# Strassen-Winograd FFN layer: token halves exchanged in the down projection, product order, hat tiles and row scaling moved

## The chip, the cores and the metric

One Trainium2 chip, one of its cores. The metric is the device time of one launch in microseconds, as the median of repeated runs. TensorE, VectorE, ScalarE, GpSimd and SyncE appear in the profile as PE (with its weight loads as PEld), DVE, ACT, POOL and SP; SP issues nearly all of the DMAs.

## The reference, cut to what matters

One decoder layer on 1024 tokens of width 1024, in float32:

```
h = h + 0.5 * post1(SwiGLU_1(pre1(h)))     FFN 1, hidden width 2816
h = h + postM(Mixer(preM(h)))              attention + linear recurrence
h = h + 0.5 * post2(SwiGLU_2(pre2(h)))     FFN 2, hidden width 2816
swiglu(x) = (silu(x @ w_gate) * (x @ w_up)) @ w_down
```

pre and post are RMS norms with a gain per column. The change touches the two FFNs, and, through one shared routine, the row scaling of the normed residual in FFN 1 and in the mixer.

## The kernel before, in words

**Products.** Every float32 product is three matmuls: each operand is split into a high half (ACT, a rounding copy, line 132) and a low half (DVE, a subtraction, line 133), and hi*hi, hi*lo, lo*hi are accumulated (lines 153 to 155). The split tiles are called hats; `wh` is a ring of 6 such tiles, `wr` a ring of 4 raw weight tiles, `hx` a ring of 6 raw hidden tiles.

**Strassen-Winograd.** Each FFN matrix product is cut in two along tokens, inner width and output width, and done in 7 products instead of 8. With A11, A12 the first and A21, A22 the second token half, and B the weight:

- s1 = A21 + A22, s2 = s1 - A11, s3 = A11 - A21, s4 = A12 - s2; t1 = B12 - B11, t2 = B22 - t1, t3 = B22 - B12, t4 = B21 - t2.
- P1 = A11 B11, P2 = A12 B21, P3 = s4 B22, P4 = A22 t4, P5 = s1 t1, P6 = s2 t2, P7 = s3 t3.
- C11 = P1 + P2, C12 = P1 + P5 + P6 + P3, C21 = P1 + P6 + P7 + P4, C22 = P1 + P5 + P6 + P7.

P1, P2 and P3 use a weight block as it is ("raw"); the others need a weight sum first (`wsum`, line 324: DVE, or DVE and POOL in turn).

**Stages.** FFN 1 runs from 0 to about 690 us, the mixer to about 1430, FFN 2 to the end. In an FFN, `hidden` (line 442) loops over 11 column tiles f and, for gate and up (m = 0, 1), over `unit` (line 380), which makes the four quarters of the hidden, S[h, j] for token half h and width half j. `early` does P1 and P2 of some units beforehand. A unit's seven products are in the order P1, P5, P2, P6, P3, P7, P4, the first two perhaps done early. P6, P7 and P4 go on in the PSUM tile `c` that P5 began. At the end the unit writes the A-operands of the down projection to DRAM: hid[0] to hid[6] hold A11, A12, s4, A22, s1, s2, s3. Before the change A11, A12 are S[0, 0], S[0, 1], and A22 is S[1, 1].

`down` (line 456) frees the pools of the hidden stage and opens its own over them; pool `hp` (`hx` and weight sums) lies where pool `xc` lay. `products` (line 480) runs P1, P2, then P5 and P6 together, P3, P7, P4, each as a loop over 11 f with 12 matmuls of 512 columns an f (24 in the P5/P6 loop). The token halves' rows are f1[0], f1[1]; L and R are their left and right 512 columns. f1[0] is complete after P3; then a generator `side` is stepped once per f beside P7 and P4: the six steps of `residual` (line 167: square on ACT, `rsqrt` on DVE and POOL, gain and addition on DVE, store, second norm with the row scaling of line 188 on DVE), and in FFN 1 eight steps of `to_T` (transposes on PE into a PSUM tile `pa`, a split each). FFN 2 ends with class `Last`: P4's weights and hats are split in the P3 and P7 loops into tiles of their own (`wl`, `xl`), and `rows` (line 592) then does P4 one 128-token tile after another, 33 matmuls each, with the post norm and the store of each beside the next.

**What sets the order.** The program is a list; the framework's list scheduler orders each engine's queue when the kernel is built, by program order and by a simulated time at which an instruction becomes ready, and adds the semaphores. A pool that lies over an older one counts as ready, for that ordering, when the older pool's last reader is through. At run time each engine, and SP with its DMAs, takes its queue strictly in order.

Of the kernel before, what the change touches and what calls it, by code (L numbers as in the profile page):

```python
# [16 lines left out]
D = 1024  # L17
# [28 lines left out]
def layer(ctx: ExitStack, tc: tile.TileContext, I: dict, out: bass.AP):  # L46
# [172 lines left out]


    hid = dram.tile([7, NP, 128, HT], F32, name="hid")
    spill = dram.tile([max(EARLY.values()), 2, 128, HT], F32, name="spill")
    spill_a = dram.tile([4, 128, 2, HT], F32, name="spill_a")
    turn = [0]

    class Ffn:
# [124 lines left out]

        def out(self, S, m, f, i, h, j, c):

# [4 lines left out]
            else:  # L358
                tt(S[h, j], S[h, j], c, op=OP.mult)
                nc.sync.dma_start(hid[i - 1, f], S[h, j])  # L360

        def early(self):

            for f in range(self.early_tiles):
# [10 lines left out]
                for m in range(2):  # L375
                    yield from self.prod_steps(2, r[m][0][:, 1], q[m], False)
                    self.out(S, m, f, 1, 0, 0, q[m])
                    yield

        def unit(self, f, m, S):  # L380

# [18 lines left out]
            if first:  # L400
                self.prod(2, b21, q, False)
                self.out(S, m, f, 1, 0, 0, q)
            else:
                if m == 0:
                    S[0, 0] = self.place(0, 0)
                    nc.sync.dma_start(S[0, 0], hid[0, f])
                yield
# [12 lines left out]
            tt(y, c, p1, op=OP.add)  # L420
            self.out(S, m, f, 4, 1, 1, y)
            t4 = self.wsum(b21, t2, OP.subtract, ESUM)
            yield
            self.prod(4, t4, c, False)
            tt(e, c, e, op=OP.add)
            if m == 0:
                nc.scalar.activation(e, e, AF.Silu)
                return
            tt(S[1, 0], S[1, 0], e, op=OP.mult)

            s1, s2, s4 = (self.at.tile([128, HT], F32, name=n) for n in ("s1", "s2", "s4"))
            s3 = S[1, 0]
# [3 lines left out]
            nc.sync.dma_start(hid[6, f], s3)  # L436
            tt(s2, s1, S[0, 0], op=OP.subtract)
            nc.sync.dma_start(hid[5, f], s2)
            tt(s4, S[0, 1], s2, op=OP.subtract)
            nc.sync.dma_start(hid[2, f], s4)  # L440

        def hidden(self):
# [3 lines left out]
            for f in range(NP):  # L446
                S = {}
                for m in range(2):
                    u = self.unit(f, m, S)
                    next(u)  # L450
# [29 lines left out]
        def products(self, f1, done, beside, last):  # L480


            Wd = self.Wd
            T2 = [self.wl.tile([128, 512], F32, name=f"t2_{f}", tag=f"xl{f}") for f in range(NP)]

# [33 lines left out]

            side = iter(())  # L520

            def raws(acc, i, b, start):
                for f in range(NP):
                    x = halves(xhat(i, f))
                    mul(acc, x, halves(blocks(f, b)[b]), f, start)

            pa = [ptile("pa") for _ in range(4)]
            raws(pa, 1, (0, 0), True)
            for t in range(4):
                nc.scalar.activation(L(1, t), pa[t], AF.Copy)  # L530
            raws(pa, 2, (1, 0), False)
            for t in range(4):
                nc.scalar.activation(L(0, t), pa[t], AF.Copy)
            pa, pb = ([ptile(tag) for _ in range(4)] for tag in ("pa", "pb"))
# [12 lines left out]
            pa = [ptile("pa") for _ in range(4)]  # L547
            for f in range(NP):
                x = halves(xhat(3, f))
                W = blocks(f, (1, 1), (1, 0)) if last else blocks(f, (1, 1))  # L550
                mul(pa, x, halves(W[1, 1]), f)
                if last:
                    last.weights(f, self.wsum(W[1, 0], T2[f], OP.subtract, 2))
            for t in range(4):
                tt(R(0, t), pa[t], R(0, t), op=OP.add)
            side = then(done(), beside)
            for f in range(NP):
                x = halves(xhat(7, f))
                W = blocks(f, (0, 1), (1, 1))
                mul(pb, x, halves(self.wsum(W[1, 1], W[0, 1], OP.subtract, 2)), f, False)  # L560
                if last:
                    last.inner(f, xhat(4, f))
                next(side, None)
            for t in range(4):
                tt(R(1, t), pb[t], R(1, t), op=OP.add)
            if last:
                last.rows(f1[0], f1[1], pb, side)
                return
            for f in range(NP):
                x = halves(xhat(4, f))  # L570
                W = blocks(f, (1, 0))
                mul(pb, x, halves(self.wsum(W[1, 0], T2[f], OP.subtract, 2)), f, False)
                next(side, None)
            run(side)
            for t in range(4):
                tt(L(1, t), pb[t], L(1, t), op=OP.add)

    class Last:
# [4 lines left out]

        def weights(self, f, s):
            w = self.w[f] = self.ffn.wl.tile([128, 2, 512], F32R, name=f"wl{f}")
            split(w[:, 0], w[:, 1], s)

        def inner(self, f, s):
            x = self.x[f] = self.ffn.wl.tile([128, 2, 512], F32R, name=f"xl{f}")
            split(x[:, 0], x[:, 1], s)  # L590

        def rows(self, x, m, acc, side):
            src, dst, g = self.ffn.src, self.ffn.dst, self.g
            run(side)
            head = []
# [10 lines left out]
            for t in range(4):  # L606
                p = acc[t]
                for f in range(NP):
                    mm3(p, cols(self.x[f], t), (self.w[f][:, 0], self.w[f][:, 1]), f == 0, f == NP - 1, False)
                L = m[t][:, :512]  # L610
# [38 lines left out]
    rp = pool(sr1, "r1")  # L649
    rows0 = [F1.xb.tile([128, D], F32, name="xrow0", tag=f"xh6_{t}") for t in range(4)]  # L650
    load_rows(rows0, 0)
# [14 lines left out]
    def to_T(pl, rows, res, tag):  # L666
        for dt in range(8):
# [8 lines left out]
    f1, res1, srp, sf1, sf0 = F1.down(lambda: xT.append(pool(sxta, "xta", side="right")),  # L676
                                      lambda rows: to_T(xT[2], rows, xT[0], "pa"))
    sf0.close()
# [641 lines left out]
```

## Time and profile before

| | |
|---|---|
| median of 3 runs | 2028.68 us (2025.11 to 2029.44) |
| the profiled execution's own time | 2022.87 us |
| its span | 2021.1 us |
| PE busy | 1914.3 us, 95% |
| DVE, ACT, POOL busy | 70%, 48%, 29% |
| mean granted TensorE clock | 0.977 |

The profile's page gives busy shares for the whole span; the questions here are about stretches of 5 to 60 us, so the trace is read by windows, by the timeline of one engine, and by tile. A granted clock of 1.00 is 2.4 GHz, 0.50 is 1.2 GHz; the mean of a window lies between when the clock was low for part of it.

### The profile page before, as it was taken

The page shows a single profiled execution, that of the slowest core. Times are in us where ns is not written, and L with a number is a line of the kernel's source. Part 1 is how long each engine was busy: PE and PEld are TensorE (multiplying, and loading weights), DVE is VectorE, ACT ScalarE, POOL GpSimd, SP SyncE. Part 2 cuts the span into 40 slices and gives each one's busy share as a digit, 9 for nine tenths or more (in the row PEclk, how much of TensorE's full clock was granted, in tenths as well). Part 3 has the DMA queues.
Part 4 walks back from the last instruction along what each step waited for, and adds up shares of the span by engine and source line. Part 5 has one row for each costly group of instructions (what it writes and reads, how often), then busy time and mean ns, then how long its engine had stood idle before and what let it go on. Part 6 is the DMA issues. An engine that isn't in the chain of part 4 may idle for free.

```text
span 2021.1 us, 26939 instructions
## 1 busy us (share of the span) xinstructions
PE 1914.3 (95%) x9034; PEld 1566.8 (78%) x9034; DVE 1413.3 (70%) x2515; ACT 966.7 (48%) x1887; POOL 579.9 (29%) x549
## 2 busy tenths in 40 slices
PE   7999999999998989899999999988989999989988
PEld 5788888877886766688787878877868888868876
DVE  5777766655759865856885785754787788756794
ACT  7423333324444536458886676754633222224451
POOL 1433212200004444155534431223233332310131
PEclk9999999999999999999999999999989999999999
DMA  6554333236859453563323253134745455457694
GB/s 218 168 157 154 102 110 110 94 108 221 287 166 309 113 164 95 153 170 87 122 93 113 87 162 123 64 113 126 241 152 162 146 163 174 135 198 255 207 308 136
DMA packets 290107, 316.54 MB, mean 157 GB/s; under 512 B 19920, under 2 KB 200240, under 8 KB 289968
## 3 DMA queue, kind: packets, MB, share of 16 engines
q1 hardware_dynamic: 289392, 312.72, 49.1%
q0 software_dynamic: 576, 2.10, 0.3%
q8 instruction: 71, 1.16, 0.2%
q14 instruction: 68, 0.56, 0.1%
HBM read 237.62 MB, written 74.97 MB: 155 GB/s over the span
## 4 chain that ended last, share of the span: by engine, by line
PE 67%; DVE 12%; DMA 8%; issue 7%; ACT 5%; POOL 1%; SPq 0%; DVEq 0%; POOLq 0%; ACTq 0%
PE pa L154 10%; PE pa L155 10%; PE pa L153 10%; PE pb L155 4%; PE pb L154 4%; PE pb L153 4%; PE pj L153 4%; PE pj L154 4%; PE pj L155 4%; PE av L1105 3%; PE pt L1118 3%; DVE wh L133 3%; DMA wr<-in_ffn_w_down 3%; PE sc L1056 1%; PE sc L1055 1%
## 5 line engine op out<-in xcount | busy, mean ns | idle before, releaser
L153 PE MATMUL pa<-xh,wh 128*128 128x512 f32 x728 | 284.7, 394 | 11.6 <-ACT xh L132 4.6
L154 PE MATMUL pa<-xh,wh 128*128 128x512 f32 x728 | 286.0, 393 | 0.7 <-DVE xh L133 0.7
L155 PE MATMUL pa<-xh,wh 128*128 128x512 f32 x728 | 281.3, 392 | 0.0
L132 ACT ACTIVATE wh<-ws 128x512 fp32r<-128x512 f32 x231 | 143.3, 626 | 267.2 <-PE pa L155 193.2
L133 DVE TENSOR_TENSOR wh<-wr,wh 128x512 fp32r<-128x512 f32 (+1 forms) x248 | 195.3, 792 | 60.2 <-ACT wh L132 59.2
L132 ACT ACTIVATE wh<-wr 128x512 fp32r<-128x512 f32 (+1 forms) x248 | 152.7, 621 | 133.8 <-PE pa L155 80.1
L324 POOL TENSOR_TENSOR ws<-wr 128x512 f32<-128x512 f32 x54 | 79.7, 1476 | 389.6 <-DVE wh L133 249.1
L133 DVE TENSOR_TENSOR wh<-ws,wh 128x512 fp32r<-128x512 f32 x231 | 188.2, 816 | 4.0 <-ACT wh L132 2.9
L132 ACT ACTIVATE wh<-hx 128x512 fp32r<-128x512 f32 x143 | 90.1, 630 | 209.6 <-PE pa L155 117.1
L153 PEld LDWEIGHTS pa<-xh,wh 128*128 128x128 f32 x728 | 137.7, 189 | 42.9 <-ACT xh L132 4.8
L1072 POOL TENSOR_SCALAR s<-s,cf 128x64 f32<-128x64 f32 (+4 forms) x192 | 117.3, 634 | 185.6 <-DVE cf L1068 127.1
L133 DVE TENSOR_TENSOR wh<-hx,wh 128x512 fp32r<-128x512 f32 x143 | 105.3, 736 | 84.6 <-ACT wh L132 84.3
L154 PEld LDWEIGHTS pa<-xh,wh 128*128 128x128 f32 x728 | 137.7, 189 | 30.3 <-DVE xh L133 1.7
L155 PEld LDWEIGHTS pa<-xh,wh 128*128 128x128 f32 x728 | 137.8, 189 | 29.2
L154 PE MATMUL pa<-wh 128*128 128x512 f32 x352 | 139.2, 395 | 4.2 <-DVE wh L133 4.2
L143 POOL TENSOR_TENSOR wh<-wr,wh 128x512 fp32r<-128x512 f32 (+1 forms) x74 | 101.9, 1388 | 137.4 <-ACT wh L142 134.5
L155 PE MATMUL pa<-wh 128*128 128x512 f32 x352 | 138.7, 394 | 0.0
L153 PE MATMUL pj<-xT,wh 128*128 128x512 f32 (+1 forms) x304 | 124.1, 412 | 13.2 <-DVE gq L913 5.1
L153 PE MATMUL pb<-xh,wh 128*128 128x512 f32 x328 | 128.9, 393 | 0.0
L155 PE MATMUL pb<-xh,wh 128*128 128x512 f32 x328 | 128.6, 393 | 0.0
L154 PE MATMUL pb<-xh,wh 128*128 128x512 f32 x328 | 128.3, 391 | 0.0
L133 DVE TENSOR_TENSOR PT<-pt,PT 128x512 fp32r<-128x512 f32 (+3 forms) x184 | 104.4, 578 | 29.4 <-ACT PT L132 28.6
(360 smaller groups left out, 4629.5 us busy)
## 6 DMA issues: line engine op xcount, KB each, us to landing
hx<-hid SPq DMA_DIRECT2D x154, 256.0 KB
wr<-in_ffn_w_down SPq DMA_DIRECT2D x132, 256.0 KB
wr<-in_ffn_w_gate SPq DMA_DIRECT2D x60, 512.0 KB
wr<-in_ffn_w_up SPq DMA_DIRECT2D x60, 512.0 KB
hid<-S SPq DMA_DIRECT2D x88, 256.0 KB
wr<-in_w_in SPq DMA_DIRECT2D x36, 512.0 KB
hid<-s SPq DMA_DIRECT2D x66, 256.0 KB
wr<-in_ffn_w_down SPq DMA_DIRECT2D x33, 512.0 KB
```

Of the source, the lines that this page charges most:

```text
L132: nc.scalar.activation(hi, src, AF.Copy)
L133: tt(lo, src, hi.bitcast(F32), op=OP.subtract)
L143: nc.gpsimd.tensor_tensor(lo, src, hi.bitcast(F32), op=OP.subtract)
L153: nc.tensor.matmul(p, a[0], b[0], start=start and fresh, stop=False, skip_group_check=not fresh)
L154: nc.tensor.matmul(p, a[0], b[1], start=False, stop=False, skip_group_check=not fresh)
L155: nc.tensor.matmul(p, a[1], b[0], start=False, stop=stop, skip_group_check=not fresh)
L324: (nc.vector if turn[0] % every == 0 else nc.gpsimd).tensor_tensor(s, a, b, op=op)
L1055: nc.tensor.matmul(p[:, :b - a], Q[:, 0, ts], rhs[:, a:b], start=True, stop=False)
L1056: nc.tensor.matmul(p[:, :b - a], Q[:, 1, ts], rhs[:, a:b], start=False, stop=True)
L1072: nc.gpsimd.tensor_scalar(S[k, br][:, :n], S[k, br][:, :n], cf[:, k, br:br + 1], 1.0, op0=OP.mult, op1=OP.mult)
L1105: nc.tensor.matmul(av[:, k0 * 128:(k0 + nk) * 128], lhs, PT[:npart, y, at:at + nk * 128], start=(wi == 0 and y == 0), stop=(wi == len(work ...
L1118: nc.tensor.transpose(pt[:npart, at:at + 128], S[k, br][:, (j - lo_) * npart:(j - lo_ + 1) * npart], idt)
```

## The change

- The token halves exchange roles in the down projection: A11, A12 are S[1, 0], S[1, 1], and A21, A22 are S[0, 0], S[0, 1]. hid[0] is written at the end of each unit; what `early` makes goes to a DRAM tensor of its own, hid0, and S[0, 0] of a unit that was not begun early is not stored.
- `products` now runs P1, (P5, P6), P7, P4, P3, P2. f1[0] is complete after P4. `side` is stepped beside P3 and P2, and `to_T` uses PSUM tiles `pb`; P3 and P2 accumulate in `pa`.
- In FFN 2, `Last.rows` finishes P2: its first 6 f run as a plain loop, the last 5 (`LATE`) are split in the P3 loop into own tiles and are done by token tile, 15 matmuls each.
- In the very last unit of the hidden stage P4 goes to a PSUM tile of its own, with one more DVE addition.
- Hats of P4's operand move from pool `xc` to `xb`, those of P6's from `xb` to `xc`.
- The row scaling of `residual` is an ACT copy with a scale instead of a DVE multiplication.

```diff
@@ residual
-                nc.vector.tensor_scalar(f[t], f[t], r[t], None, op0=OP.mult)
+                nc.scalar.activation(f[t], f[t], AF.Copy, scale=r[t])
@@ build1
-                self.hat(self.xc, 4, k, B[k + 4])
+                self.hat(self.xb, 4, k, B[k + 4])
...
-                self.hat(self.xb, 6, k, s2)
+                self.hat(self.xc, 6, k, s2)
@@ out
-                nc.sync.dma_start(hid[i - 1, f], S[h, j])
+                if to is not None:
+                    nc.sync.dma_start(to, S[h, j])
@@ unit
-            self.out(S, m, f, 2, 0, 1, x)
+            self.out(S, m, hid[3, f], 0, 1, x)
...
-            self.out(S, m, f, 4, 1, 1, y)
+            self.out(S, m, hid[1, f], 1, 1, y)
+            if last:
+                tt(e, c, e, op=OP.add)
+                c = either(self.tags)
             t4 = self.wsum(b21, t2, OP.subtract, ESUM)
             yield
-            self.prod(4, t4, c, False)
+            self.prod(4, t4, c, last)
             tt(e, c, e, op=OP.add)
+            self.out(S, m, hid[0, f], 1, 0, e)
...
-            nc.gpsimd.tensor_tensor(s1, S[1, 0], S[1, 1], op=OP.add)
+            nc.gpsimd.tensor_tensor(s1, S[0, 0], S[0, 1], op=OP.add)
...
-            nc.gpsimd.tensor_tensor(s3, S[0, 0], S[1, 0], op=OP.subtract)
+            nc.gpsimd.tensor_tensor(S[0, 0], S[1, 0], S[0, 0], op=OP.subtract)
...
-            tt(s2, s1, S[0, 0], op=OP.subtract)
+            tt(s2, s1, S[1, 0], op=OP.subtract)
...
-            tt(s4, S[0, 1], s2, op=OP.subtract)
+            tt(s4, S[1, 1], s2, op=OP.subtract)
@@ products (after the P5/P6 loop; the new order)
             for t in range(4):
-                tt(R(1, t), pa[t], L(1, t), op=OP.add)
+                tt(R(0, t), pa[t], L(1, t), op=OP.add)
             for t in range(4):
-                tt(R(0, t), pb[t], R(1, t), op=OP.add)
...
+                tt(R(1, t), pb[t], R(0, t), op=OP.add)
             for f in range(NP):
                 x = halves(xhat(7, f))
                 W = blocks(f, (0, 1), (1, 1))
                 mul(pb, x, halves(self.wsum(W[1, 1], W[0, 1], OP.subtract, 2)), f, False)
...
             for t in range(4):
-                tt(R(1, t), pb[t], R(1, t), op=OP.add)
...
+                tt(R(0, t), pb[t], R(0, t), op=OP.add)
             for f in range(NP):
                 x = halves(xhat(4, f))
                 W = blocks(f, (1, 0))
                 mul(pb, x, halves(self.wsum(W[1, 0], T2[f], OP.subtract, 2)), f, False)
+            for t in range(4):
+                tt(L(0, t), pb[t], L(1, t), op=OP.add)
+            side = then(done(), beside)
+            pa = [ptile("pa") for _ in range(4)]
+            late = range(NP - LATE if last else NP, NP)
+            for f in range(NP):
+                mul(pa, halves(xhat(3, f)), next_w((1, 1), f), f)
+                if f in late:
+                    last.ready(f, xhat(2, f), blocks(f, (1, 0))[1, 0])
+                next(side, None)
+            for t in range(4):
+                tt(R(1, t), pa[t], R(1, t), op=OP.add)
+            pa = [ptile("pa") for _ in range(4)]
+            for f in range(late[0] if last else NP):
+                mul(pa, halves(xhat(2, f)), next_w((1, 0), f), f)
                 next(side, None)
             run(side)
+            if last:
+                last.rows(f1[0], f1[1], pa, late)
+                return
             for t in range(4):
-                tt(L(1, t), pb[t], L(1, t), op=OP.add)
+                tt(L(1, t), pa[t], L(1, t), op=OP.add)
```

## Rows read from the trace of the kernel before

**Rows 1.** The profile's page, part 1: busy us (share of the span) xinstructions.

```profile
span 2021.1 us, 26939 instructions
...
PE 1914.3 (95%) x9034; PEld 1566.8 (78%) x9034; DVE 1413.3 (70%) x2515; ACT 966.7 (48%) x1887; POOL 579.9 (29%) x549
```

**Rows 2.** Windows of 25 us; the columns are named in the first line.

```profile
core 0: us, PE busy (x) PEld busy (x) DVE busy (x) ACT busy (x) POOL busy (x), PEclk, DMA share, GB/s
425.00:450.00 25.00, 24.12 (x106) 19.51 (x105) 11.48 (x18) 4.91 (x8) 0.51 (x1) 1.00 0.30 102
450.00:475.00 25.00, 21.11 (x83) 16.39 (x82) 13.89 (x20) 9.11 (x16) 3.50 (x2) 0.86 0.79 263
...
600.00:625.00 25.00, 23.42 (x103) 18.73 (x102) 20.14 (x29) 11.74 (x22) 8.84 (x7) 1.00 0.92 313
625.00:650.00 25.00, 19.39 (x85) 14.84 (x84) 24.85 (x35) 14.04 (x26) 12.01 (x9) 0.98 0.88 298
...
675.00:700.00 25.00, 21.32 (x82) 16.95 (x81) 19.37 (x39) 9.59 (x18) 14.71 (x14) 0.86 0.26 64
...
1775.00:1800.00 25.00, 18.70 (x70) 14.01 (x69) 14.52 (x20) 5.54 (x10) 2.87 (x2) 0.86 0.69 243
...
1925.00:1950.00 25.00, 25.00 (x112) 20.71 (x111) 22.19 (x33) 16.30 (x29) 7.89 (x5) 1.00 0.90 307
1950.00:1975.00 25.00, 19.39 (x76) 14.85 (x75) 25.00 (x36) 12.36 (x24) 8.33 (x7) 0.93 0.89 301
1975.00:2000.00 25.00, 23.71 (x105) 19.32 (x104) 10.20 (x19) 5.49 (x14) 5.59 (x5) 1.00 0.48 158
```

**Rows 3.** Timeline of PE where the hidden stage ends: start, us, operation, [idle before <-releaser].

```profile
449.33 0.47 PE L153 MATMUL pa<-xh,wh 128*128 128x512 f32 x1 [0.88 <-DVE cy L420]
...
454.35 1.91 PE L153 MATMUL pa<-wh 128*128 128x512 f32 x4 [2.05 <-ACT wh L132]
458.10 0.80 PE L154 MATMUL pa<-wh 128*128 128x512 f32 x1 [1.84 <-DVE wh L133]
...
1778.85 0.47 PE L153 MATMUL pa<-xh,wh 128*128 128x512 f32 x1 [0.87 <-DVE cx L410]
```

**Rows 4.** Timeline of SP's DMA queue at the same two places.

```profile
438.30 11.97 SPq L360 DMA_DIRECT2D hid<-S  x3
450.35 2.77 SPq L507 DMA_DIRECT2D hx<-hid  x6
...
1783.74 2.78 SPq L507 DMA_DIRECT2D hx<-hid  x6
```

**Rows 5.** Timeline of PE in P4, at the mixer's first matmul, and in P7.

```profile
649.57 0.77 PE L153 MATMUL pb<-wh 128*128 128x512 f32 x1 [4.05 <-DVE f L565]
...
687.54 0.77 PE L153 MATMUL pj<-xT,wh 128*128 128x512 f32 x1 [3.67 <-DVE f L576]
...
1962.05 0.50 PE L154 MATMUL pb<-wh 128*128 128x512 f32 x1 [3.29 <-DVE wh L133]
```

**Rows 6.** Line 188, row scaling: ns min/median/max; then what its engine waited for.

```profile
L188 DVE TENSOR_SCALAR f<-f,r x8: 737/752/1789, 633.2 to 727.8; 128x1024 f32<-128x1024 f32 x8
...
L188 DVE TENSOR_SCALAR xrow<-xrow,r x4: 745/752/756, 1416.8 to 1437.1; 128x1024 f32<-128x1024 f32 x4
...
  DMA h<-xrow: 6.2, 2
```

**Rows 7.** Tile m: ScalarE's square over rows of 1024.

```profile
L127 ACT ACTIVATE junk<-m x8: 1044/1049/1059, 1151.8 to 1176.0; 128x1024 bf16<-128x1024 f32 x8
```

**Rows 8.** Tile hx: the two halves of a split.

```profile
L132 ACT ACTIVATE wh<-hx x143: 612/632/655, 453.1 to 1976.3; 128x512 fp32r<-128x512 f32 x143
L133 DVE TENSOR_TENSOR wh<-hx,wh x143: 675/687/1790, 453.8 to 1976.9; 128x512 fp32r<-128x512 f32 x143
```

**Rows 9.** Timeline of DVE after the last matmuls: first and last step of the last token tile.

```profile
2013.67 0.69 DVE L611 TENSOR_TENSOR f<-pb,f 128x512 f32<-128x512 f32 x1 [3.10 <-PE pb L155]
...
2016.64 1.41 DVE L620 SCALAR_TENSOR_TENSOR f<-f,r,f 128x512 f32<-128x512 f32 x2 [0.66 <-POOL r L617]
```

More of the change, by code (lines that the diff above doesn't have):

```diff
@@ L39 @@
 XS, CA, HX = 3, 3, 6
+LATE = 5
 ESUM = 2
@@ L221, in layer @@
     hid = dram.tile([7, NP, 128, HT], F32, name="hid")
+    hid0 = dram.tile([max(EARLY.values()), 128, HT], F32, name="hid0")
     spill = dram.tile([max(EARLY.values()), 2, 128, HT], F32, name="spill")
@@ L350, in place, with out @@
             return (self.ap if (h, j) == (0, 0) else self.at).tile([128, HT], F32, name=f"S{h}{j}", bufs=2)
-        def out(self, S, m, f, i, h, j, c):
+        def out(self, S, m, to, h, j, c):
             if m == 0:
@@ L376, in early, with unit @@
                     yield from self.prod_steps(2, r[m][0][:, 1], q[m], False)
-                    self.out(S, m, f, 1, 0, 0, q[m])
+                    self.out(S, m, hid0[f], 0, 0, q[m])
                     yield
-        def unit(self, f, m, S):
+        def unit(self, f, m, S, last):
             r = self.load(m, f)
@@ L401, in unit @@
                 self.prod(2, b21, q, False)
-                self.out(S, m, f, 1, 0, 0, q)
+                self.out(S, m, None, 0, 0, q)
             else:
@@ L405, in unit @@
                     S[0, 0] = self.place(0, 0)
-                    nc.sync.dma_start(S[0, 0], hid[0, f])
+                    nc.sync.dma_start(S[0, 0], hid0[f])
                 yield
@@ L448, in hidden @@
                 for m in range(2):
-                    u = self.unit(f, m, S)
+                    u = self.unit(f, m, S, (f, m) == (NP - 1, 1))
                     next(u)
@@ L483, in products @@
             Wd = self.Wd
-            T2 = [self.wl.tile([128, 512], F32, name=f"t2_{f}", tag=f"xl{f}") for f in range(NP)]
+            T2 = [self.wl.tile([128, 512], F32, name=f"t2_{f}") for f in range(NP)]
             def block(r, n, k, j, f):
@@ L518, in R, with next_w @@
                 return f1[h][t][:, 512:1024]
[L520 to L525, printed above, removed]
+            def next_w(b, f):
+                return halves(blocks(f, b)[b])
             pa = [ptile("pa") for _ in range(4)]
-            raws(pa, 1, (0, 0), True)
+            for f in range(NP):
+                mul(pa, halves(xhat(1, f)), next_w((0, 0), f), f)
             for t in range(4):
                 nc.scalar.activation(L(1, t), pa[t], AF.Copy)
-            raws(pa, 2, (1, 0), False)
-            for t in range(4):
-                nc.scalar.activation(L(0, t), pa[t], AF.Copy)
             pa, pb = ([ptile(tag) for _ in range(4)] for tag in ("pa", "pb"))
@@ L543, in products @@
             for t in range(4):
-                tt(R(1, t), pa[t], L(1, t), op=OP.add)
+                tt(R(0, t), pa[t], L(1, t), op=OP.add)
             for t in range(4):
-                tt(R(0, t), pb[t], R(1, t), op=OP.add)
[L547 to L556, printed above, removed]
+                tt(R(1, t), pb[t], R(0, t), op=OP.add)
             for f in range(NP):
@@ L560, in products @@
                 mul(pb, x, halves(self.wsum(W[1, 1], W[0, 1], OP.subtract, 2)), f, False)
-                if last:
-                    last.inner(f, xhat(4, f))
-                next(side, None)
             for t in range(4):
-                tt(R(1, t), pb[t], R(1, t), op=OP.add)
-            if last:
-                last.rows(f1[0], f1[1], pb, side)
-                return
+                tt(R(0, t), pb[t], R(0, t), op=OP.add)
             for f in range(NP):
@@ L582, in __init__, with ready, rows @@
             self.ffn, self.rp, self.g, self.x, self.w = ffn, rp, g, {}, {}
[L584 to L592, printed above, removed]
+        def ready(self, f, x, w):
+            for to, s, n in ((self.x, x, "xl"), (self.w, w, "wl")):
+                to[f] = self.ffn.wl.tile([128, 2, 512], F32R, name=f"{n}{f}")
+                split(to[f][:, 0], to[f][:, 1], s)
+        def rows(self, x, m, acc, late):
             src, dst, g = self.ffn.src, self.ffn.dst, self.g
-            run(side)
             head = []
@@ L607, in rows @@
                 p = acc[t]
-                for f in range(NP):
-                    mm3(p, cols(self.x[f], t), (self.w[f][:, 0], self.w[f][:, 1]), f == 0, f == NP - 1, False)
+                for f in late:
+                    mm3(p, cols(self.x[f], t), (self.w[f][:, 0], self.w[f][:, 1]), False, f == NP - 1)
                 L = m[t][:, :512]
@@ L649, in layer @@
     rp = pool(sr1, "r1")
-    rows0 = [F1.xb.tile([128, D], F32, name="xrow0", tag=f"xh6_{t}") for t in range(4)]
+    rows0 = [F1.xb.tile([128, D], F32, name="xrow0", tag=f"xh3_{t}") for t in range(4)]
     load_rows(rows0, 0)
@@ L676, in layer @@
     f1, res1, srp, sf1, sf0 = F1.down(lambda: xT.append(pool(sxta, "xta", side="right")),
-                                      lambda rows: to_T(xT[2], rows, xT[0], "pa"))
+                                      lambda rows: to_T(xT[2], rows, xT[0], "pb"))
     sf0.close()
```

6 lines of the change are left out of this document (2 added, 4 removed).

## The prediction, made before the changed kernel was run

> **What bounds the kernel.** The page comes first: PE is busy for 1914.3 us of a span of 2021.1 [rows 1], so no change of order can be worth more than the 107 us in which PE stands still, plus what its clock loses. Next come windows of 25 us. An undisturbed one holds 112 matmuls of 512 columns (1925 to 1950, [rows 2]), one per 25/112 = 0.223 us, so a window with fewer has lost (112 - x)/112 of 25 us, be it to idleness or to the granted clock. The down projections and their edges lose:
>
> - **A1**, end of FFN 1's hidden stage, 425 to 475: 106 and 83 matmuls, 1.3 + 6.5 = 7.8 us.
> - **A2**, the same place in FFN 2, 1775 to 1800: 70 matmuls, 9.4 us.
> - **B**, P7 and P4 of FFN 1, 600 to 650: 103 matmuls, 2.0 us; the next window holds short transposes, so there I take its idle time, 25 - 19.39 = 5.6, and 2% of clock, 0.5: together 8.1 us.
> - **C**, the mixer's first matmuls, 675 to 700: 82 matmuls, 6.7 us.
> - **D**, P7 of FFN 2, 1950 to 2000: 76 and 105 matmuls, 8.0 + 1.6 = 9.6 us.
>
> That is 41.6 us; the change aims at nothing else of PE's. The timelines tell what came last. In A, PE waits 0.88 us for the read of `c` before P4 may go on in it, then 2.05 and 1.84 us for P1's first hats [rows 3]. These are late because their `hx` loads stand in SP's queue behind a store of hid that waits for the last unit, 12 us for three stores, and go out only at 450.35 [rows 4]. In B the 4.05 us wait is for the additions after P7, in D the 3.29 us wait for a low half [rows 5], and DVE is busy for 24.85 and 25.00 of 25 us there [rows 2]: it is the bound. In C PE waits 3.67 us for the last additions, which free the PSUM tiles that the mixer takes over [rows 5]. In A and C the granted clock averages 0.86 over the window [rows 2], 7 of 25 us at 1.2 GHz after the idle time; that half-speed stretch is within the counts above.
>
> **The change part by part.**
>
> *Hats at other places, P4 of the last unit in its own tile.* `hp` lies over `xc`. Before, `xc` holds hats of P4, the last product of the hidden stage, and so the scheduler has `hx` ready only when all is over; afterwards `xc` holds the hats of P5 and P6, which in the last unit are followed by P3, P7 and P4, 36 matmuls of 0.223 = 8.0 us. Six loads need 2.77 us to issue [rows 4], a first split 0.63 + 0.69 [rows 8]: they fit in 8.0. The 0.88 us wait goes with the fresh tile; it costs one more DVE addition of 0.69 us on an engine that is half idle there (11.48 of 25, [rows 2]). Between nothing and all of it, I take nearly all, the loads having room: A1 keeps 0.8 and gives 7.0 us. A2 has a further wait of 0.87 us on `cx` [rows 3], which the change doesn't touch, and keeps 1.8: 7.6 us.
>
> *Residual beside raw products.* A weight sum every other f leaves DVE in the stretch beside `side` (about 9 f in 25 us, 4.7 sums of 0.69 = 3.2 us), in FFN 1 also four scalings of 0.75 = 3.0 [rows 6], and POOL's sums go, beside which a low half takes up to 1.79 instead of 0.69 us [rows 8]. From 24.85 DVE falls under 19 us of 25. P7 and P4 keep their sums with nothing beside them: 2 x 0.69 + 0.35 = 1.73 of 2.68 us an f. Four more additions of 0.69 fall at changes of product, where P7 now follows P6 in the same tiles `pb`; the first is read 2 us before the last is written, so I cost it at nothing, 2.8 us if that cover fails. What is late next is ACT in the first six f, and DMA, at 298 to 313 GB/s and 0.9 of its share already [rows 2]. B gives between nothing and 8.1; I take two thirds, 5.4 us.
>
> *D.* DVE also loses the 11 `xl` low halves, 0.69 each, and gains 10 late ones, all in the last five f: 4 x 0.69 = 2.8 of 2.68 us, no slack for 13 us. I leave 4.0 us there: gain 5.6, between -4 and 9.6.
>
> *C.* The mixer's `pj` and `pt` lie over `pb`, which is now only used by transposes long over; the additions on `pa` no longer hold PE. Between 0 and 6.7 us; I take 4.7, because the mixer's DVE work after it starts no earlier and part of the lead will be waited out again.
>
> *Row scaling on ACT.* 16 tiles (two residuals of FFN 1, two of the mixer): 0.75 us on DVE [rows 6], on ACT not shown for a float32 copy; the nearest row is the square of the same 1024 columns, 1.05 us [rows 7]. I take that. ACT in 625 to 650 goes from 14.04 to at most 14.04 + 4 x 1.05 = 18.2 of 25. The scaling also waits for the store of the same tile: DVE stood 6.2 us for two of them [rows 6]. Now ACT stands, and high halves queue behind. For the mixer's second half, where PE has no spare hats, I charge 0.5 us. The Trainium skill ("ScalarE: Activation LUTs", Rules for kernel authors) says that a multiplication belongs on VectorE. By its figures an estimate is 1.13 us a tile instead of 1.05, 1.3 us more for ACT over the kernel; the sum stays, but the rule's warning is the third rival.
>
> *Tail.* A token tile's last part shrinks from 33 to 15 matmuls, 7.4 to 3.3 us, while its chain on DVE from first addition to last store takes 2016.64 + 1.41 - 2013.67 = 4.4 us [rows 9], with holes that the next tile can fill. Between 0 and 3 x 1.1 = 3.3 us for four tiles; I take 0.7, DVE's own work being less than 3.3.
>
> *At nothing:* 16 more stores of 256 KB in the hidden stages (22 of S[1, 0], less 6 of S[0, 0]), one DMA issue each on SP beside 600 us of matmuls; s1 no longer waits for S[1, 0].
>
> **Sum:** 7.0 + 7.6 + 5.4 + 5.6 + 4.7 - 0.5 - 0.7 = 29.1 us, from the profiled execution's 2022.87 to 1993.8. The median of the runs shown is 0.29% above that execution; in the same ratio, 1999.5 us.
>
> **The rivals.**
>
> 1. *The loads stay behind a store* (14%). hid[0] of the last unit is now stored after P4, later than the store that held the loads. If the scheduler puts it ahead of them, P1 starts some 4 us later than now, in both FFNs, and A is lost: 29.1 - 14.6 - 8 = 6.5 us gained, 2022. For it: SP's queue is strictly in order [rows 4]. Against: six tiles are ready 8 us earlier.
> 2. *DMA is the bound of FFN 2's P3* (14%). The late f load two blocks and two hats, 1.05 MB in 2.68 us, 391 GB/s, where the busiest of these windows shows 313 [rows 2]. Five f then take 17 us, not 13.4, with 4 MB of residual traffic in front of them. D gives nothing, or loses 4: 2005 to 2009. The Trainium skill ("DMA: Bandwidth & Descriptors", Bandwidth) has about 358 GB/s as the HBM limit of a core; by that five f take 14.6 us, and the rival is worth 1.2 instead of 3.6 us.
> 3. *Slower: ACT stands for the stores* (7%). Each of 16 scalings may wait as two did, 3.1 us [rows 6], with the high halves of PE's next tiles behind it in ACT's queue: 50 us of waiting. PE's lead is the `wh` ring, three f; the rival decides where over 29.1/50 = 58% reaches PE. At 70%, 35 us: 2034. For it: DMA at 0.9 of its share in B makes stores land late. Against: ACT is idle for half of the span [rows 1].
> 4. *The lead is waited out* (5%). The stages after the down projections wait for DVE again and little remains: 2026.
>
> **How the numbers follow.** 60% go to the forecast, 1999.5, by itself 1988 to 2010 (the bounds above, which don't fall together). A measurement of this kernel can tell 0.2%, 4 us, from no change. Faster: the first case, rival 2, most of rival 1: 0.86. Same: the rest of rival 1, half of rival 4: 0.07. Slower: rival 3: 0.07. The range goes from 1985, everything won, to 2018; it leaves out rival 3, rival 4 and most of rival 1.
>
> **What would show it.** Right: SP issues six `hx` loads before the last unit's P4, and the windows at A hold over 105 matmuls with a clock of 1.00; DVE is under 22 of 25 us beside the residual; the mixer's first `pj` matmul follows P2 within 1 us. Wrong: `hx` behind the store of hid[0] (rival 1); waits on `hx` or `wr` in FFN 2's P3 (rival 2); ACT idle for `h<-f` with PE idle behind it (rival 3); longer waits between 690 and 860 us (rival 4).

## The result, and the profile after

The changed kernel took 1999.51 us (median of 4 runs, 1995.48 to 2002.93) where the kernel before took 2027.64 (4 runs): ratio 0.9861, 95% interval [0.9838, 0.9885]. The forecast was 1999.5, in a range of 1985 to 2018. The profiled execution took 1997.58 us, with a span of 1995.8 instead of 2021.1, 25.3 us less, and a mean granted clock of 0.983.

The page of the changed kernel, part 1, has the busy times:

```profile
span 1995.8 us, 26985 instructions
...
PE 1904.1 (95%) x9034; PEld 1560.1 (78%) x9034; DVE 1372.5 (69%) x2509; ACT 979.5 (49%) x1895; POOL 566.4 (28%) x549
```

PE does the same 9034 matmuls, DVE 41 us less and ACT 13 us more. Where the time came from is seen by cutting the span at starts of matmuls in PE's timeline (before, 454.35 and 687.54 are in [rows 3] and [rows 5]):

| stretch, us | before | after | difference |
|---|---|---|---|
| start to FFN 1's first P1 matmul | 454.4 | 450.0 | -4.4 |
| to the mixer's first `pj` matmul | 233.2 | 219.5 | -13.7 |
| to the first score matmul | 202.4 | 198.3 | -4.1 |
| to the last score matmul | 433.0 | 438.5 | +5.5 |
| to FFN 2's first P1 matmul | 465.0 | 458.2 | -6.8 |
| to the end of the last matmul | 225.8 | 223.3 | -2.5 |

Windows of 25 us of the changed kernel, with the columns of [rows 2]:

```profile
425.00:450.00 25.00, 25.00 (x111) 20.48 (x110) 12.84 (x19) 7.74 (x13) 1.66 (x1) 1.00 0.53 174
450.00:475.00 25.00, 25.00 (x111) 20.45 (x110) 16.36 (x25) 9.76 (x18) 1.81 (x1) 1.00 0.81 275
...
600.00:625.00 25.00, 24.98 (x113) 20.38 (x112) 19.36 (x31) 16.73 (x32) 3.25 (x6) 1.00 0.67 222
625.00:650.00 25.00, 24.75 (x122) 19.91 (x121) 19.86 (x33) 18.53 (x32) 3.84 (x5) 1.00 0.77 266
650.00:675.00 25.00, 25.00 (x111) 20.59 (x110) 14.67 (x36) 13.29 (x24) 10.08 (x11) 1.00 0.62 178
675.00:700.00 25.00, 25.00 (x108) 20.06 (x108) 14.51 (x14) 15.29 (x26) 20.56 (x17) 1.00 0.90 255
...
1450.00:1475.00 25.00, 18.03 (x69) 13.51 (x68) 24.13 (x27) 9.93 (x18) 14.68 (x10) 0.86 0.63 200
1475.00:1500.00 25.00, 25.00 (x112) 20.71 (x111) 19.57 (x26) 7.16 (x12) 8.19 (x6) 1.00 0.41 127
...
1750.00:1775.00 25.00, 25.00 (x112) 20.71 (x111) 17.80 (x27) 8.71 (x15) 3.47 (x2) 1.00 0.67 230
...
1925.00:1950.00 25.00, 21.36 (x86) 16.89 (x85) 19.76 (x30) 11.42 (x21) 2.84 (x2) 0.93 0.95 340
1950.00:1975.00 25.00, 21.77 (x93) 16.83 (x92) 15.20 (x23) 10.75 (x22) 6.26 (x4) 1.00 0.47 179
```

Where the hidden stages end (425 to 475 and 1750 to 1775), PE is never idle and the clock stays at 1.00, against 21.11 busy us and 0.86 in [rows 2]. Beside the residual (600 to 650) DVE falls from 24.85 to under 20 of 25 us and PE loses 0.3 us. But FFN 2's P3 and P2 (1925 to 1975) have 86 and 93 matmuls, as poor as P7 and P4 were before (76 and 105 in 1950 to 2000, [rows 2]). What PE waits for, in its timeline:

```profile
485.02 0.50 PE L155 MATMUL pb<-wh 128*128 128x512 f32 x1 [2.47 <-DVE wh L134]
...
544.43 0.47 PE L154 MATMUL pb<-wh 128*128 128x512 f32 x1 [1.50 <-DVE f L545]
...
715.50 0.79 PE L154 MATMUL pj<-tl,gw 128*128 128x512 f32 x1 [6.01 <-DVE tl L137]
...
1152.52 0.47 PE L1052 MATMUL sc<-KA,Q 128*128 128x128 f32 x1 [2.10 <-DVE nmax L1056]
...
1857.28 0.47 PE L154 MATMUL pb<-wh 128*128 128x512 f32 x1 [0.90 <-DVE f L545]
...
1943.38 1.29 PE L154 MATMUL pa<-wh 128*128 128x512 f32 x4 [3.56 <-ACT wh L133]
1952.51 1.20 PE L154 MATMUL pa<-wh 128*128 128x512 f32 x4 [1.78 <-ACT wh L133]
1956.70 0.47 PE L154 MATMUL pa<-wh 128*128 128x512 f32 x1 [1.17 <-DVE f L567]
```

The waits of [rows 3] and [rows 5] are gone. The lines at 544 and 1857 are the additions between P6 and P7; the last three stand in FFN 2's P3 and at its end. ACT's timeline says what ACT itself waited for just before:

```profile
1942.69 0.63 ACT L133 ACTIVATE wh<-wr 128x512 fp32r<-128x512 f32 x1 [3.77 <-DMA wr<-in_ffn_w_down]
...
1951.83 0.63 ACT L133 ACTIVATE wh<-wr 128x512 fp32r<-128x512 f32 x1 [3.81 <-DMA wr<-in_ffn_w_down]
```

A weight load, while the DMA engines are busy for 0.95 of the window at 340 GB/s. The timeline of SP's queue at the end of FFN 1's hidden stage:

```profile
435.60 10.77 SPq L512 DMA_DIRECT2D hx<-hid  x7
446.66 0.32 SPq L364 DMA_DIRECT2D hid<-S  x1
```

Seven `hx` loads go out before the last unit's stores, behind one of which they stood in [rows 4].

### The profile page after: what moved, and what is told of

Read it like the earlier page. It is cut to its first block, busy times and chain, and to the rows that moved or that the text cites. A ratio compares the mean times of both kernels' runs of the same rounds, so it can differ in the third digit from the quotient of the medians.

```text
span 1995.8 us, 26985 instructions
## 1 busy us (share of the span) xinstructions
PE 1904.1 (95%) x9034; PEld 1560.1 (78%) x9034; DVE 1372.5 (69%) x2509; ACT 979.5 (49%) x1895; POOL 566.4 (28%) x549
## 5 line engine op out<-in xcount | busy, mean ns | idle before, releaser
L133 ACT ACTIVATE wh<-ws 128x512 fp32r<-128x512 f32 x242 | 150.7, 626 | 263.4 <-PE pb L156 149.5
L154 PE MATMUL pb<-xh,wh 128*128 128x512 f32 x592 | 230.3, 392 | 3.8 <-ACT wh L133 3.8
L155 PE MATMUL pb<-xh,wh 128*128 128x512 f32 x592 | 231.6, 391 | 0.4 <-DVE xh L134 0.4
L156 PE MATMUL pb<-xh,wh 128*128 128x512 f32 x592 | 226.9, 391 | 2.8 <-DVE wh L134 2.8
L134 DVE TENSOR_TENSOR wh<-wr,wh 128x512 fp32r<-128x512 f32 (+1 forms) x243 | 181.3, 750 | 67.4 <-ACT wh L133 66.4
L154 PE MATMUL pa<-xh,wh 128*128 128x512 f32 x464 | 181.4, 394 | 5.5 <-ACT xh L133 4.4
L155 PE MATMUL pa<-xh,wh 128*128 128x512 f32 x464 | 182.1, 392 | 0.7 <-DVE xh L134 0.7
L156 PE MATMUL pa<-xh,wh 128*128 128x512 f32 x464 | 180.5, 392 | 0.0
L154 PEld LDWEIGHTS pb<-xh,wh 128*128 128x128 f32 x592 | 111.6, 188 | 28.6 <-ACT wh L133 4.7
L156 PEld LDWEIGHTS pb<-xh,wh 128*128 128x128 f32 x592 | 111.5, 188 | 27.3 <-DVE wh L134 3.5
L155 PE MATMUL pa<-wh 128*128 128x512 f32 x332 | 131.0, 394 | 0.9 <-DVE wh L134 0.8
L155 PEld LDWEIGHTS pb<-xh,wh 128*128 128x128 f32 x592 | 111.5, 188 | 24.4 <-DVE xh L134 0.8
L156 PE MATMUL pa<-wh 128*128 128x512 f32 x332 | 130.1, 392 | 0.0
```

What stands on the lines that cost most here:

```text
L133: nc.scalar.activation(hi, src, AF.Copy)
L134: tt(lo, src, hi.bitcast(F32), op=OP.subtract)
L154: nc.tensor.matmul(p, a[0], b[0], start=start and fresh, stop=False, skip_group_check=not fresh)
L155: nc.tensor.matmul(p, a[0], b[1], start=False, stop=False, skip_group_check=not fresh)
L156: nc.tensor.matmul(p, a[1], b[0], start=False, stop=stop, skip_group_check=not fresh)
```

## The experiments

Each is the changed kernel with the edit shown: first those on what made the gain, then those on what took part of it back. Stretches are cut as in the table above.

**Hats back in their old pools.**

```diff
-                self.hat(self.xb, 4, k, B[k + 4])
+                self.hat(self.xc, 4, k, B[k + 4])
...
-                self.hat(self.xc, 6, k, s2)
+                self.hat(self.xb, 6, k, s2)
```

> The hats of P4 and P6 go back to their old pools; all else stays as changed. Theory: the loss at the end of the two hidden stages (7.8 and 9.4 us before, nothing in the changed kernel) comes back nearly whole, because the hx loads go out only when P4 is over; the span grows by 12 to 17 us, the first P1 matmul of the down projections follows its last P4 matmul by 1.5 us or more, and the clock falls to 1.2 GHz there. Rival: the tile of its own for the last P4 did it; then the span stays within 3 us.

Measured: 1998.06 us (one run, as in most of these experiments). P1 starts 2.6 us later, at 452.6; from there the mixer takes 219.6 us as before the edit, and FFN 2's P1 follows the last score after 458.6 us (458.2): most of the gain stays. The queue of SP in this kernel:

```profile
448.45 0.36 SPq L512 DMA_DIRECT2D hx<-hid  x1
...
450.10 3.00 SPq L512 DMA_DIRECT2D hx<-hid  x6
```

The first load goes out 1.9 us earlier than the 450.35 of [rows 4], the other six about as late as there. In both kernels P1's first matmul starts 4.0 to 4.1 us after the first load (450.35 to 454.35 and 448.45 to 452.56). With P4 in its own tile the pause of 0.88 us is gone too, so PE waits only 0.59 and 0.68 us there, and the clock stays at 1.00. The pools of the hats alone are not the cause; but 2.6 us are lost here without them.

**The last unit's own PSUM tile taken back.**

```diff
-                    u = self.unit(f, m, S, (f, m) == (NP - 1, 1))
+                    u = self.unit(f, m, S, False)
```

> P4 of the very last unit goes on in the tile of P6 and P7 again; hats stay moved. With the hats alone back the span did not change, so either the own tile or something else of the change keeps the end of the hidden stages free. Theory now: the two are each enough, since both bring the hx loads out of the place behind the last stores; then this costs 1 to 2 us an FFN (the 0.9 us wait for the read of c) and the span grows by 2 to 4 us. Rival: the own tile alone did it; then 6 to 9 us an FFN come back, 12 us or more in all.

Measured: 1994.41 us; the 2 to 4 us that the theory adds didn't come. Seven `hx` loads go out from 435.89 on, as in the changed kernel, and P1 begins at 447.5, ahead of the hidden stage's last matmuls at 454.1: the loads being early, matmuls of P1 fill the hole of 0.88 us that P4 leaves. The own tile alone isn't the cause either.

**Both back, and the scaling on DVE**: the order of the products alone is left of the change's main parts.

```diff
the two edits above, and
-                nc.scalar.activation(f[t], f[t], AF.Copy, scale=r[t])
+                nc.vector.tensor_scalar(f[t], f[t], r[t], None, op0=OP.mult)
```

> Hats back, own tile back, row scaling back on DVE: what is left is the exchange of the token halves and the order of the products. Theory (either of two is enough at the end of the hidden stages): that loss comes back now, 6 to 9 us an FFN, and the span is 2005 to 2013 us; from the first P1 matmul of FFN 1 to the mixer's first the gain stays but for the slow clock after the transition. Rival (the exchange of roles itself frees it, since the store of the last P7 result no longer stands ahead of the loads): the span stays under 2000 us.

Measured: 2018.61 us, span 2016.7, slower than the theory's 2005 to 2013. PE's timeline has the waits of [rows 3] again:

```profile
449.58 0.47 PE L154 MATMUL pa<-xh,wh 128*128 128x512 f32 x1 [0.88 <-DVE cy L424]
454.92 1.88 PE L154 MATMUL pa<-wh 128*128 128x512 f32 x4 [2.36 <-ACT wh L133]
457.82 0.79 PE L155 MATMUL pa<-wh 128*128 128x512 f32 x1 [1.03 <-DVE wh L134]
```

SP's queue sends the first `hx` loads as late as in [rows 4], and the window after them has as few matmuls as in [rows 2]:

```profile
450.93 1.94 SPq L512 DMA_DIRECT2D hx<-hid  x4
...
450.00:475.00 25.00, 21.61 (x83) 16.77 (x82) 13.99 (x21) 9.11 (x16) 1.79 (x1) 0.86 0.81 268
```

So hats or tile, each alone, keep the gain at A or nearly all of it, and without either it is lost: 106 and 83 matmuls in 425 to 475, the 7.8 us of before, and 76 in 1775 to 1800, 8.0 us. In stretches this kernel is 10.4 us behind at the mixer's first `pj` (679.84 to 669.45), 7.2 more between the last score and FFN 2's P1 (465.34 to 458.16), and 3.6 after it (226.91 to 223.27). Of the 10.4 not all is A's: PE also waits 1.35 and 0.70 us at 645, beside the residual, and the clock is 0.93 in 625 to 650. The scaling, which is also undone here, is priced by the next run and by the last ones.

**The row scaling alone back on DVE** (the third edit above).

> Only the row scaling goes back to DVE. Theory: in FFN 1's P3 and P2 DVE has room (it is busy 19 of 25 us), so this costs PE 0 to 3 us there, and the span changes by less than 4 us. Rival (ACT stands for the stores): the attention's stretch, from the first score matmul to the last, which is 5.5 us longer in the changed kernel (438.5 against 433.0), comes back to 433, and the span falls by 4 us or more.

Measured: 1993.82 us. From P1 to the mixer 219.5 us as with ACT; two waits of 0.84 and 0.70 us stand at 635. The rival looks all but met: the scores take 434.6 us and the span falls by 3.9; the last runs take it up again. In the changed kernel itself the rows of line 189 give what ACT's copy takes and waited for:

```profile
L189 ACT ACTIVATE f<-f,r x8: 1136/1152/1158, 621.8 to 706.8; 128x1024 f32<-128x1024 f32 x8
...
  DMA h<-f: 9.5, 6
  POOL r L122: 3.3, 2
  DMA h<-xrow: 1.8, 2
```

1.15 us a tile, and 9.5 + 1.8 us of ACT's time for eight stores, beside 3.3 for two reciprocal roots on POOL; of that two waits of 0.3 us reached weight loads of PE.

**The mixer's PSUM lists exchanged**, so that its first `pj` tiles lie over `pa`, which P2's additions read last.

```diff
-    psum(eps_, "pse", dict(sc=SC, av=AV), dict(pj=PJ, pt=PT_))
+    psum(eps_, "pse", dict(pj=PJ, pt=PT_), dict(sc=SC, av=AV))
```

> The mixer's PSUM pools change places: its projections (pj, pt) lie over pa, the accumulators of the last product, its scores over pb. Theory: the mixer's first matmul waits for the last additions of the down projection again, 1 to 4 us of PE idle there, up to 3.4 more by the clock; from the first P1 matmul of FFN 1 to the first score matmul the time grows by 2 to 7 us. Rival: with DVE relieved the additions come at once, and it makes no difference over 1 us.

Measured: 1991.14 us. P1 to the first score takes 416.7 us, in the changed kernel 417.8: at C, the place of `pj` isn't what counts. What is left of its cause is DVE, no longer full (24.85 to under 20 us of 25) when the last additions come; in this kernel it stands ready for them and does them at once:

```profile
666.77 2.48 DVE L577 TENSOR_TENSOR f<-pa,f 128x512 f32<-128x512 f32 x4 [3.81 <-PE pa L156]
```

The total, 8.4 us under the changed kernel's median, is taken up with the last runs.

**A weight sum for every f beside the residual of FFN 1** (it computes P3 and P2 with other weights).

```diff
+            def with_sum(b, f):
+                return halves(self.wsum(blocks(f, b)[b], T2[f], OP.subtract, 2))
...
-                mul(pa, halves(xhat(3, f)), next_w((1, 1), f), f)
+                mul(pa, halves(xhat(3, f)), next_w((1, 1), f) if last else with_sum((1, 1), f), f)
...
-                mul(pa, halves(xhat(2, f)), next_w((1, 0), f), f)
+                mul(pa, halves(xhat(2, f)), next_w((1, 0), f) if last else with_sum((1, 0), f), f)
```

> In FFN 1 P3 and P2 get a weight sum each f, as P7 and P4 had beside the residual before (the weight block less T2, so FFN 1's left columns and P3's part are other numbers); nothing else. Theory (DVE beside the residual was the bound, and its backlog held the mixer's start too): from the first P1 matmul of FFN 1 to the mixer's first matmul the time grows from 219.5 us by 6 to 12 us, with DVE over 23 of 25 us beside the residual. Rival (the order or the place of the residual did it, not the sums): under 2 us.

Measured: 2005.68 us, span 2003.9; P1 to the mixer 226.4 us, 6.9 more. Four timelines of this kernel (SP, DVE, ACT, PE) show one chain:

```profile
610.50 0.33 SPq L512 DMA_DIRECT2D hx<-hid  x1
617.60 0.33 SPq L492 DMA_DIRECT2D wr<-in_ffn_w_down  x1
618.02 0.38 SPq L178 DMA_DIRECT2D xres<-in_x  x1
...
623.01 1.23 DVE L183 TENSOR_TENSOR f<-f,xres 128x1024 f32<-128x1024 f32 x1 [6.46 <-DMA xres<-in_x]
...
624.29 1.15 ACT L189 ACTIVATE f<-f,r 128x1024 f32<-128x1024 f32 x1 [7.28 <-DMA h<-f]
...
625.49 0.66 PE L164 MATMUL pb<-idt,f 128*128 128x128 f32 x4 [3.73 <-ACT f L189]
```

The residual's own load stands in SP's queue behind a weight load that goes out 7 us after the one before it; DVE waits for the load, ACT for the store, PE for ACT. What SP itself waited for, and POOL's timeline:

```profile
SPq L492 <- POOL ws L327: 6.7, 1, 6.7
...
611.16 7.66 POOL L327 TENSOR_TENSOR ws<-wr,t 128x512 f32<-128x512 f32 x2 [2.08 <-DVE wh L134]
```

The weight load waited 6.7 us for a weight sum on POOL, which reads a tile of the ring that the load refills. That sum's record is 6.4 us long, where the median of these sums is 1.3; POOL's records are rough, and why this one is long stays open. The sums beside the residual cost nearly what the change saves there (7.8 us in windows), but not by filling DVE, as the theory had it: DVE stood, and was busy for 17.4 and 22.5 of 25 us in 600 to 625 and 625 to 650. So this run shows that the sums cost that much beside the residual; that they cost it before by a full DVE rests on [rows 2] and [rows 5].

**The late loads of FFN 2 left out** (the last five f of P2 are computed with P3's operands).

```diff
-                mul(pa, halves(xhat(3, f)), next_w((1, 1), f), f)
+                x, w = xhat(3, f), blocks(f, (1, 1))[1, 1]
+                mul(pa, halves(x), halves(w), f)
                 if f in late:
-                    last.ready(f, xhat(2, f), blocks(f, (1, 0))[1, 0])
+                    last.ready(f, x, w)
```

> In FFN 2's P3 loop the five late f of P2 load nothing: the same number of splits is made from P3's own hidden tile and weight block, so P2's last five f are computed with P3's operands; the ten loads of 256 KB are left out. Theory (DMA is the bound there): the waits of 3.56 and 1.78 us in that loop go, and from the first P1 matmul of FFN 2 to the last matmul the time falls from 223.3 us by 5 to 9 us. Rival (DVE and ACT, four splits an f, are the bound): the waits stay, the time moves by less than 2 us.

Measured: 1997.53 us; FFN 2 takes 222.2 us from P1 to the end instead of 223.3, which isn't the theory's 5 to 9 us less; the waits didn't stay either, as the rival had it. The waits on ACT in the P3 loop are gone, so the loads made them; two for low halves, of 0.47 and 0.74 us, are left. But another appears in PE's timeline, at the change to P2, and DVE's timeline has its reason:

```profile
1955.42 0.77 PE L154 MATMUL pa<-wh 128*128 128x512 f32 x1 [4.48 <-DVE f L568]
...
1952.24 1.22 DVE L183 TENSOR_TENSOR f<-f,xres 128x1024 f32<-128x1024 f32 x1 [2.82 <-DMA xres<-h]
```

The additions that free `pa` begin at 1954.59, behind this addition of the residual in DVE's queue, and it stood 2.82 us for a load of its own. This one wait of PE's is 4.48 us, where the three of the changed kernel were 6.51. The ten late low halves in five f show only as the 1.2 us within the loop.

**The late operands readied beside P4**, for f = 2, 4, 6, 8, 10, from the weight block that P4 has loaded anyway, and thus spread over 11 f and without five loads.

```diff
+            late = range(2, NP, 2) if last else ()
             for f in range(NP):
                 x = halves(xhat(4, f))
                 W = blocks(f, (1, 0))
                 mul(pb, x, halves(self.wsum(W[1, 0], T2[f], OP.subtract, 2)), f, False)
+                if f in late:
+                    last.ready(f, xhat(2, f), W[1, 0])
...
-                if f in late:
-                    last.ready(f, xhat(2, f), blocks(f, (1, 0))[1, 0])
...
-            for f in range(late[0] if last else NP):
+            for f in (f for f in range(NP) if f not in late):
```

> A version meant to be better: the late f of P2 in FFN 2 are 2, 4, 6, 8, 10, split in the P4 loop, where their weight block is loaded anyway: 1.3 MB of loads left out, 1.3 MB and ten splits taken out of P3. Theory (DMA first, then DVE, hold FFN 2's P3): the waits of 3.6, 1.8 and 1.2 us there shrink to under 3 us together, from the first P1 matmul of FFN 2 to the last the time falls from 223.3 to 216 to 219 us, and the launch takes 1992 to 1996 us. Rival: P4 has no room for it (DVE 1.7 + 0.7 of 2.7 us an f) and the loss moves there; no gain.

Measured: 1994.46 us (4 runs, 1992.35 to 1995.1), ratio to before 0.9845 [0.9826, 0.9864]; P1 to the end takes 217.0 us, 6.3 less. Its window and its remaining waits on PE:

```profile
1925.00:1950.00 25.00, 25.00 (x112) 20.64 (x111) 20.43 (x31) 13.60 (x25) 4.26 (x4) 1.00 0.82 276
...
1892.53 0.47 PE L154 MATMUL pb<-wh 128*128 128x512 f32 x1 [3.03 <-DVE f L551]
...
1954.47 0.47 PE L154 MATMUL pa<-wh 128*128 128x512 f32 x1 [1.80 <-DVE f L567]
```

This is what the theory forecast. P3 runs with 112 matmuls at 0.82 of DMA. A wait of 3.03 us for additions between P7 and P4 is what it pays.

**Three kernels on one chip**: the changed kernel again; the late operands beside P4 with the lists exchanged; the same operands with the scaling on DVE.

> The changed kernel as it is, beside the two below on one chip. Theory (the mixer's attention stretch is set by the order that the scheduler happened to write, here with a stand of DVE near 1150 us): it stays 4 to 8 us behind kernels whose order lacks that stand; 1996 to 2002 us. Rival (the 4 to 8 us between these kernels are spread between executions and chips): its median comes within 2 us of the medians of the two others plus what their last down projections differ by.

> Late operands of P2 readied beside P4 from the block already loaded, and the two PSUM lists of the mixer's stage exchanged. Its engine queues are those of the run with the exchanged lists up to FFN 2's last down projection. Theory: the parts add up: 1991.1 less 3.0 (FFN 2's down projection 217.0 instead of 220.0 us) = 1988 us, the stretch from the first to the last score product 434 to 437 us. Rival (spread between executions): that stretch anywhere from 434 to 441, the median 1988 to 1995.

> The same late operands beside P4, and the row scaling of the residual back on VectorE. Its engine queues are those of the run with the scaling on VectorE up to FFN 2's last down projection. Theory: 1993.8 less 5.8 (217.0 instead of 222.8 us) = 1988 us, the score stretch 433 to 436 us. Rival (spread between executions): 1988 to 1994; then the scaling's engine is worth nothing, by neither sign.

| kernel | us | first to last score | FFN 2's P1 to the end |
|---|---|---|---|
| the change again | 1999.50 (1992.98 to 2001.76) | 440.6 | 222.6 |
| beside P4, lists exchanged | 1986.18 (1984.98 to 1987.93) | 433.1 | 215.5 |
| beside P4, scaling on DVE | 1994.49 (1993.68 to 1995.37) | 437.7 | 218.1 |

The second beats both kernels: its ratio to before (2023.85 us here) is 0.9807 [0.9788, 0.9826], and its slowest run lies under the changed kernel's fastest. Its medians add up: the operands beside P4 are worth 5.0 us with either list (1999.5 to 1994.46, 1991.14 to 1986.18), the exchange 8.4 and 8.3. But these pairs are of different chips, 1991.14 is a single run, and the third kernel, which missed its theory's 1988 us, doesn't fit: with the scaling on DVE the operands change the total from 1993.82 to 1994.49. The stretch that the operands touch is steadier than the totals: FFN 2 from P1 to the end is 4.5 to 6.3 us shorter in all three pairs (223.3 to 217.0, 220.0 to 215.5, 222.9 to 218.1).

The scaling's engine is worth nothing that these runs can tell (third kernel against the operands beside P4 alone: 1994.49 and 1994.46 us, ratios to before 0.9847 and 0.9845, each known to about 0.002 or 4 us), not the 5.7 us that the single run promised. With the same engine queues in that stretch, its scores took 434.6 us once and 437.7 once. So some 3 us there are spread between executions. Four executions in the changed kernel's order (twice itself, the operands beside P4, the late loads left out) took 438.5, 440.6, 441.2 and 439.0 us, the two with the lists exchanged 435.4 and 433.1; the gap of 3 us or more between the two groups is put down to the order. PE's timeline of the change again, then of the second kernel:

```profile
1153.95 0.33 PE L1052 MATMUL sc<-KA,Q 128*128 128x128 f32 x1 [2.09 <-DVE nmax L1056]
```

```profile
1154.71 0.78 PE L1115 MATMUL pt<-idt,s 128*128 128x128 f32 x4 [1.25 <-DVE PT L134]
```

The wait of 2.1 us stands in all four executions of that order, in both of the changed kernel with 256 and 254 matmuls in 1150 to 1200 and a clock of 0.93 in both; with the lists exchanged it is not there, and the same 50 us hold 281 at 0.97. What made it is in DVE's timeline of the changed kernel: the norm of the mixer's residual, written ahead of a score's maximum, stood for a reciprocal root on POOL.

```profile
1150.57 1.28 DVE L180 SCALAR_TENSOR_TENSOR m<-m,r,gpost 128x1024 f32<-128x1024 f32 x1 [1.40 <-POOL r L122]
```

This wait is not the whole of it: the third kernel has no wait like it there, yet 261 matmuls in the same 50 us, a clock of 0.93 and scores of 437.7 us. Why exchanged lists lead the scheduler to another order there wasn't tried further.

## Why the prediction was right, and where its steps were not

The total was met to 0.1 us, but that is luck: misses in both directions cancelled. Of the 29.1 us that the sum forecast for the profiled execution, 25.3 came; and the median, taken as 0.29% above that execution, lay 0.10% above it (1999.51 to 1997.58). Counted in windows as the prediction counted them, for the span:

- **A1** gave 7.4 for 7.0, **A2** 9.4 for 7.6: right. SP, the windows and the clock show what "what would show it" asked for, and rival 1 is out. The prediction gave the hats nearly all and the tile 0.9 us; the runs show that the hats alone keep all of it, the tile alone all but 2.6 us of A1 and 1.3 of A2 (106 matmuls in 1750 to 1775). A further gain wasn't in the sum: FFN 2's first unit has 69 and 112 matmuls in 1450 to 1500, 3.6 us better than before:

```profile
1450.00:1475.00 25.00, 21.48 (x82) 16.81 (x81) 24.71 (x31) 12.09 (x23) 11.82 (x8) 0.87 0.47 143
1475.00:1500.00 25.00, 21.71 (x83) 17.17 (x82) 19.81 (x22) 7.34 (x13) 11.02 (x8) 0.86 0.55 173
```

  Before, PE had two long waits there, 3.52 us before 1469.25 and 3.29 before 1489.81, and the clock was low after each; in the changed kernel the long waits, 3.84 and 2.77 us, stand within 4 us of each other, and the clock is low once. The gain is lost again in the kernel with both edits undone (79 and 84); its cause is open.
- **B** gave 7.8 for 5.4: "I take two thirds" was too careful. DVE at 19.36 and 19.86 us is a little over the forecast of under 19, and nothing came in its place; ACT at 18.53 meets the bound of 18.2 almost.
- **C** gave 5.6 for 4.7 in its windows; the mixer's next wait grew from 5.1 to 6.01 us, part of the lead waited out as written. Its reason failed: the sum named the PSUM tiles under `pj`, and the run with the exchanged lists shows no difference. In its place stands DVE, ready for the last additions when they come.
- **D** is the term that failed. "I leave 4.0 us there: gain 5.6" became a loss of 0.4 (45 matmuls missing in 1925 to 1975, 10.0 us against 9.6). Rival 2, at 14%, is what happened in this stretch: five f load 1.05 MB each, and DMA stood at 0.95 of its share. Its price, "nothing, or loses 4", was right. The forecast priced DVE's 2.8 of 2.68 us an f and treated DMA as a rival, though both were near their limit: the late f ask for 391 GB/s, and the most that 25 us moved in any of these runs is 387 (1925 to 1950, lists exchanged). The run without the loads found an addition of the residual right behind, which stood for a load, and 1.2 us for low halves. The Trainium skill ("DMA: Bandwidth & Descriptors", Bandwidth) has about 358 GB/s as a core's HBM limit; the changed kernel stays under it here with 340, but the 387 GB/s, loads and stores together, are above it, and the measurement decides.
- **P6 to P7.** "I cost it at nothing, 2.8 if that cover fails": it failed in both FFNs, 1.50 + 0.90 = 2.4 us. DVE's timeline of the changed kernel shows why:

```profile
541.20 1.28 DVE L543 TENSOR_TENSOR f<-pa,f 128x512 f32<-128x512 f32 x2
542.40 0.68 DVE L134 TENSOR_TENSOR wh<-hx,wh 128x512 fp32r<-128x512 f32 x1
543.00 0.68 DVE L134 TENSOR_TENSOR wh<-ws,wh 128x512 fp32r<-128x512 f32 x1
543.60 2.48 DVE L545 TENSOR_TENSOR f<-pb,f 128x512 f32<-128x512 f32 x4
```

  The 2 us of lead were there, but two low halves of P7's operands (1.2 us) stand between the additions of `pa` and the one that frees `pb`. The prediction compared when the tiles are ready, not what else DVE's queue has between.
- **P5's start.** A wait of 2.47 us at 485, some 1.4 more than the like one before (1.12 us before 522.26), was in no step.
- **Row scaling.** 1.15 us a tile for 1.05; the charge of 0.5 and rival 3 were not borne out: ACT stood 1.4 us for each of eight stores, not 3.1 for each of 16, and almost none of it reached PE. Its chain does exist: with sums beside the residual it cost PE 3.73 us at one place. The Trainium skill ("ScalarE: Activation LUTs", Rules for kernel authors) puts multiplications on VectorE; the runs with the scaling on either engine (1994.46 and 1994.49 us) show no price for the other choice. By the Trainium skill's figures in that section, 0.3 us and 0.83 ns an element, the estimate is 1.15 us, not the 1.13 that the prediction gives; the trace has 1.15.
- **Tail.** Charged 0.7; last matmul to the end of the span went from 7.5 to 8.1 us. Right.
- **The scores**, 5.5 us slower, were in no term. The change touches them only by the scaling of the residual beside their second half; their queues are re-ordered all the same, and in this order DVE stood for POOL, which is part of it; up to 3 of the 5.5 us can be spread between executions.

In sum, 7.4 + 9.4 + 3.6 + 7.8 + 5.6 - 0.9 - 0.4 - 2.4 - 1.4 - 5.5 - 0.6 = 22.6 of the 25.3 us. The other 2.7 are not one small remainder: by the table of stretches, 22.2 us are won up to the first score, where these terms make 17.0, and 9.3 are won after the last, where they make 11.7. Part of the first is in 650 to 675, a window that no term of the prediction counted (clock 0.95 before, 1.00 after). Windows of two kernels don't begin at the same instruction, so terms read from them are good to a few us at best.

## What to carry to other kernels

Before operands are readied beside a product, count both budgets of that stretch, DMA bytes and the splitting engine's time per step; where both are near their limit, ready them where the block is loaded anyway. When a scheduler writes the order, an edit shifts queues hundreds of microseconds away: cut the span at fixed instructions and compare every stretch, so that a gain isn't credited, or a loss charged, to the wrong edit. A gain that either of two edits keeps is seen only when both are undone.

## What had not been expected

- A single run's 5.7 us for the scaling's engine vanished in a pair of four runs each (1994.49 and 1994.46): one run can't price 5 us here, although the four runs lie within 3 us in either kernel.
- Exchanging two PSUM lists, which changes no instruction's work, goes with 8.3 us, 0.4% (operands beside P4 in both): four runs of either kernel, on two chips, with ratios to before of 0.9845 [0.9826, 0.9864] and 0.9807 [0.9788, 0.9826]. 8.1 us of it lie in the scores (441.2 to 433.1), and some 3 there can be spread.
